# A decoder trunk's first mixer: VectorE's work in a written-out order, x loaded first, subtractions moved off GpSimd

## The chip, the cores and the metric

The kernel runs on one core of one Trainium2 chip. A core has five engines with an instruction queue each: TensorE (PE in the profile; PEld is its weight load) multiplies matrices into PSUM; VectorE (DVE) and ScalarE (ACT) work element by element and may read PSUM; GpSimd (POOL) does so on SBUF alone; SyncE (SP) issues DMA loads and stores, as the others also can. An engine runs its own queue in order and waits for the others by semaphores. The metric is device time in microseconds (us): the median of several runs; lower is better.

## The reference, cut to what matters

The program is a trunk of two decoder layers over 1024 tokens of width 1024, all in float32. Each layer is a mixer and an MLP, and in front of each stands an RMSNorm whose result is scaled and shifted by vectors made from a conditioning vector c:

```python
cond = jax.nn.silu(c)
mod = cond @ w_ada[i] + b_ada[i]                      # 6 vectors of 1024 per layer
sh1, sc1, gt1, sh2, sc2, gt2 = jnp.split(mod, 6, axis=-1)
h = rmsnorm(x, g) * (1.0 + sc1) + sh1
# layer 0's mixer (latent attention)
cq  = rmsnorm(h @ w_dq, g_q)                          # 384 wide
ckv_kr = h @ w_dkv                                    # 256 of a latent, 64 of a key
ckv, k_rope = rmsnorm(ckv_kr[..., :256], g_kv), rope(ckv_kr[..., 256:], positions)
q  = (cq @ w_uq)   # 8 heads, 128 plain + 64 rotary
kv = (ckv @ w_ukv) # 8 heads, 128 of a key + 128 of a value
```

Causal attention and an output product follow, then the MLP; layer 1 has a sliding-window mixer. The change lies in the way from x, c and the weights to the first heads of layer 0: the first mixer's entrance.

## The kernel before, in words

Activations lie transposed: a tile has 128 of the 1024 channels on its partitions and 512 tokens (half of them) along it, so h is eight chunks d = 0 to 7 for each of two halves. Precision near float32 comes from pairs: `split` rounds a tile to a TensorE type (the high part, a copy on ScalarE, mostly) and subtracts it from the source (the rest, one subtraction); `mm` then does three products, high by high, high by rest and rest by high. So every operand of a product costs a copy and a rest on some engine.

The entrance, in `run`: loads of constants, x's first half (four loads of 512 KB), and, one set per chunk, two tiles of w_ada and one of w_down (768 wide). VectorE multiplies a w_ada tile by the row of cond and adds it up along the row (`ada_sum`, L391): a column of the modulation; two columns and `ada_finish` (L399, L402) give a chunk's shift and gain. x is squared on ScalarE (L448), the squares added on VectorE (L452), and `rstd` (L461 to L468) sums over the channels by a product with ones on TensorE, then takes a logarithm and an exponential on ScalarE and a correction on VectorE: the factor. Each chunk of the first half is normed by `modulated` (VectorE times the factor, L481; ScalarE scale and shift, L482; ScalarE rounds; GpSimd takes the rest, L192), its weights are split by `down_weights` (the rest on VectorE for k = 0, 2, 4, on GpSimd otherwise, L224 for odd k), and 18 products go into six PSUM banks: three tiles of the query latent (0, 1, 2), two of the key and value latent (3, 4), one of the rotary key (5). The second half's x is loaded at k = 2, squared at k = 4, its factor made at k = 6, and its eight chunks are normed after the loop, ahead of the first half's latents.

`mla` then makes the first half's latents (each with an `rstd` of its own) and key rotation, multiplies the second half's eight chunks by tiles 5, 4, 3, later 2, 0 and 1, with the first pieces between: R (rotary queries, `mla_rope`), V (values), P (a head's plain queries and keys, `mla_head`). What comes later of these pieces is given out by `Fill`, which lets pieces run step by step in front of the score unit where they are due. Weights that come later are loaded by `Weights` and split by `weights` (rest on GpSimd). The remaining columns of w_ada trickle in between the score units.

What sets the order: the program is written in one stream, and a planner puts each engine's queue in order by a simulated time, a higher place in the stream first among what is ready. So instructions of an engine need not keep the written order, unless `chain` ties them: before, that is done for SyncE's loads and for ScalarE up to the end of the first half's loop. VectorE's order is the planner's. Buffers come in rings by tag (`t`: eight tiles of 512 for temporaries, `w`: four for raw weights, `s`: 42, PSUM `S` 3, `T` 3, `A` 2), and `chain_slots` makes the first writes into a ring keep the written order.

## Time and profile before

| What | us |
|---|---|
| median of 3 runs (lowest, highest) | 2151.04 (2149.67, 2151.49) |
| profiled execution, its span | 2150.22, 2148.4 |
| TensorE busy | 2039.0 (95%) |
| VectorE busy | 1649.7 (77%) |
| ScalarE busy | 1105.5 (51%) |
| GpSimd busy | 378.1 (18%) |

The span runs from the first to the last instruction; the profiled execution is 1.8 us longer than its span. Busy times are sums of the instructions' durations with overlaps counted once; a product's end is modelled, so a busy TensorE need not be at its peak. Where an instruction follows another on its engine at once, the next one's start minus its own is what it costs there; the duration shown is a little longer. The granted clock of TensorE is a share of 2.4 GHz; the trace holds no record of it before about 36 us and shows 1.00 there.

### The profile page before, as it was taken

To read this page: it belongs to the slowest core of one execution; us is meant where nothing else is said; L and a number is where in the kernel's file an instruction comes from. 1 tells how busy PE (TensorE), PEld (TensorE's weight loads), DVE (VectorE), ACT (ScalarE), POOL (GpSimd) and SP (SyncE) were. 2 spreads that over 40 slices of the span, in tenths; PEclk is the share of its full clock that TensorE was granted. 3 is DMA by queue.
4 is the path that set the end of the run, shared out by engine and by line. 5 is a ranking of instruction groups with operands and counts; after the bars stand their busy time and mean duration, and the time that the engine had idled before them with its cause. 6 is when DMAs were issued, how large, how long until landed. Compare 5 with 4: busy or idle time off the path is not lost.

```text
span 2148.4 us, 28329 instructions
## 1 busy us (share of the span) xinstructions
PE 2039.0 (95%) x10256; PEld 1718.5 (80%) x10256; DVE 1649.7 (77%) x2747; ACT 1105.5 (51%) x1934; POOL 378.1 (18%) x360
## 2 busy tenths in 40 slices
PE   5889999999999999999998999999999999999996
PEld 3667888889788887788887888889888887788885
DVE  8897676638887775998798998967966555987796
ACT  4455556535655554443254567855655554433443
POOL 4422222230000000000022777730000000000002
PEclk9999999999999999999998999999899999999998
DMA  8233221162566667654442122362364437634522
GB/s 301 62 112 95 57 84 35 59 196 79 207 226 225 244 246 290 244 178 166 172 154 69 60 79 70 101 187 77 129 224 156 160 125 305 218 131 150 176 79 79
DMA packets 135981, 322.61 MB, mean 150 GB/s; under 512 B 12657, under 2 KB 61313, under 8 KB 135842
## 3 DMA queue, kind: packets, MB, share of 16 engines
q1 hardware_dynamic: 135474, 320.48, 42.7%
q8 instruction: 80, 1.31, 0.3%
q14 instruction: 59, 0.48, 0.1%
q0 software_dynamic: 80, 0.14, 0.0%
q10 hardware_dynamic: 288, 0.20, 0.0%
HBM read 236.61 MB, written 84.15 MB: 149 GB/s over the span
## 4 chain that ended last, share of the span: by engine, by line
PE 74%; DVE 14%; ACT 4%; issue 3%; DMA 3%; POOL 2%; SPq 0%; DVEq 0%; POOLq 0%; ACTq 0%
PE S L230 28%; PE A L230 20%; PE T L230 19%; DVE s L192 4%; DMA w<-w_ada 1%; PE S L1238 1%; PE T L1267 1%; POOL s L192 1%; ACT s L189 1%; PE T L1000 1%; PE A L461 1%; DVE t L481 1%; DVE t L477 1%; DVE w L391 1%; DVE s L191 1%
## 5 line engine op out<-in xcount | busy, mean ns | idle before, releaser
L230 PE MATMUL S<-s,s 128*128 128x512 f32 (+3 forms) x3464 | 782.5, 379 | 14.3 <-DVE s L192 5.9
L230 PEld LDWEIGHTS S<-s,s 128*128 128x128 f32 x3464 | 626.4, 191 | 133.9 <-DVE s L192 9.1
L230 PE MATMUL A<-s,s 128*128 128x512 f32 (+3 forms) x3072 | 628.1, 354 | 17.6 <-DVE s L192 5.8
L230 PEld LDWEIGHTS A<-s,s 128*128 128x128 f32 x3072 | 500.3, 191 | 97.6 <-DVE s L192 9.5
L230 PE MATMUL T<-s,s 128*128 128x512 f32 (+1 forms) x2352 | 522.8, 378 | 24.9 <-ACT s L189 14.7
L230 PEld LDWEIGHTS T<-s,s 128*128 128x128 f32 x2352 | 420.4, 191 | 113.6 <-ACT s L189 18.6
L189 ACT CAST s<-s 128x1024 fp32r<-128x1024 f32 (+2 forms) x324 | 273.7, 899 | 309.6 <-DVE s L699 160.7
L192 DVE TENSOR_TENSOR s<-s,s 128x1024 fp32r<-128x1024 f32 (+2 forms) x316 | 325.8, 1063 | 13.8 <-ACT s L189 12.0
L192 POOL TENSOR_TENSOR s<-w,s 128x1024 fp32r<-128x1024 f32 (+3 forms) x53 | 124.3, 2352 | 671.8 <-ACT s L189 670.9
L189 ACT CAST s<-w 128x1024 fp32r<-128x1024 f32 (+3 forms) x184 | 171.3, 949 | 21.9 <-DVE w L522 5.0
L192 DVE TENSOR_TENSOR s<-w,s 128x1024 fp32r<-128x1024 f32 (+2 forms) x131 | 139.8, 1087 | 50.6 <-ACT s L189 49.3
L650 DVE TENSOR_TENSOR t<-S,t 128x512 f32<-128x512 f32 x96 | 65.8, 687 | 115.8 <-PE S L230 115.8
L651 ACT ACTIVATE t<-t 128x512 f32<-128x512 f32 x96 | 60.6, 632 | 128.4 <-DVE t L650 128.4
L1437 POOL TENSOR_TENSOR s<-s,t 128x256 f32<-128x256 f32 (+1 forms) x10 | 11.5, 1175 | 640.1 <-PE S L230 632.5
L779 DVE SCALAR_TENSOR_TENSOR s<-S,mod,s 128x512 f32<-128x512 f32 (+1 forms) x102 | 72.5, 715 | 41.3 <-PE S L230 40.9
L192 DVE TENSOR_TENSOR s<-T,s 128x512 fp32r<-128x512 f32 (+2 forms) x156 | 91.6, 602 | 12.6 <-ACT s L189 12.2
L391 DVE SCALAR_TENSOR_TENSOR s<-s,s 128x1024 f32<-128x1024 f32 x72 | 90.6, 1271 | 10.9 <-DMA s<-w_ada 10.6
L189 ACT CAST s<-T 128x512 fp32r<-128x512 f32 (+2 forms) x156 | 76.1, 523 | 42.8 <-PE T L1267 21.6
L605 DVE TENSOR_TENSOR s<-s,s 128x1024 f32<-128x1024 f32 x64 | 77.0, 1221 | 16.4 <-DMA t<-s 13.0
L985 POOL TENSOR_SCALAR s<-s,n 128x128 f32<-128x128 f32 (+3 forms) x64 | 51.0, 798 | 184.8 <-DVE n L984 162.2
L652 ACT ACTIVATE s<-t 128x512 f32<-128x512 f32 x128 | 79.7, 630 | 2.7
L699 DVE TENSOR_TENSOR s<-s,s 128x1024 f32<-128x1024 f32 x64 | 77.5, 1216 | 0.2
(151 smaller groups left out, 2048.7 us busy)
## 6 DMA issues: line engine op xcount, KB each, us to landing
t<-s SPq DMA_DIRECT2D x112, 512.0 KB, 2.8
s<-t SPq DMA_DIRECT2D x112, 512.0 KB, 5.2
s<-w_ada SPq DMA_DIRECT2D x72, 512.0 KB, 6.5
w<-w_ff SPq DMA_DIRECT2D x64, 512.0 KB, 4.4
s<-w_ff SPq DMA_DIRECT2D x64, 512.0 KB, 5.2
w<-w_ada SPq DMA_DIRECT2D x24, 512.0 KB, 3.6
w<-w_qkv SPq DMA_DIRECT2D x20, 512.0 KB, 3.5
w<-w_o SPq DMA_DIRECT2D x16, 512.0 KB, 3.5
```

The costliest lines, as they stand in the source:

```text
L189: he.copy(hi, src)
L191: he.tensor_copy(hi, src)
L192: le.tensor_tensor(out=lo, in0=src, in1=hi.bitcast(F32), op=ALU.subtract)
L230: self.nc.tensor.matmul(ps, lhsT=a, rhs=b, start=first and i == 0, stop=last and i == 2, skip_group_check=more)
L391: self.nc.vector.scalar_tensor_tensor(out=t, in0=t, scalar=1.0, in1=cond, op0=ALU.mult, op1=ALU.mult, accum_out=self.mod[layer][:, c:c + 1])
L605: nc.vector.tensor_tensor(out=out, in0=x, in1=y, op=ALU.subtract)
L650: nc.vector.tensor_tensor(out=v, in0=ps, in1=v, op=ALU.add)
L651: nc.scalar.activation(v, v, AF.Relu)
L652: nc.scalar.activation(q[r, z][:, a * HALF:(a + 1) * HALF], v, AF.Square)
L699: nc.vector.tensor_tensor(out=out, in0=x, in1=y, op=how)
L779: ins = nc.vector.scalar_tensor_tensor(out=t, in0=ps, scalar=self.modcol(layer, 5, d), in1=t, op0=ALU.mult, op1=ALU.add).ins
L985: nc.gpsimd.tensor_scalar(out=s[:, :W], in0=s[:, :W], scalar1=sm, scalar2=1.0, op0=ALU.mult, op1=ALU.mult)
```

## The change

x's four loads stand in front of everything on SyncE, and the five constants are loaded from ScalarE's queue. Twelve products of a tile of ones by itself are put on TensorE at the start. `squares` makes all squares first and adds only some of them (three at the first half, four at the second), and hands the others to `rstd` as they are. The raw w_down tile is loaded with the two w_ada tiles of its chunk. The first half's loop is written anew, with `first_norm` in three steps (product with the factor; ScalarE makes the high part and the full value in two passes; VectorE takes the rest), all of w_down's rests on VectorE, and VectorE's instructions from the squares on tied in the written order, like ScalarE's from the start. The second half's x is loaded at k = 3, squared and added at k = 4 to 6.

In `mla` the second half's chunks are normed by the same `first_norm`, one at a time, each followed by its products with tiles 3 and 4, and the first half's latents and key rotation stand between chunks 1 and 2, 2 and 3, 4 and 5. Tiles 5, 2, 0, 1 follow; P of head 0 comes before tile 0, V after it, and P of head 1 in front of the second half's query latent. The rests of w_vr, w_qk and w_o0 and the rotary product in `mla_rope` go from GpSimd to VectorE, the scale of the sine table to ScalarE.

```diff
@@ weights
-        self.split(t, w, nc.scalar, nc.gpsimd)
+        self.split(t, w, nc.scalar, nc.gpsimd if name in ("w_qkv", "w_v", "w_o1") else nc.vector)
@@ down_weights
-        le = nc.vector if k % 2 == 0 and k < 6 else nc.gpsimd
+        le = nc.vector
@@ setup
-        self.cT, _ = ld(nc.sync, "cT", [P, ND])
-        self.vec, _ = ld(nc.sync, "vec", [P, 66])
-        self.positions, first = ld(nc.scalar, "positions", [P, 256], I32)
-        self.ident, second = ld(nc.scalar, "ident", [P, P])
-        self.b_ada, _ = ld(nc.sync, "b_ada", [P, 96])
+        self.cT = ld(nc.scalar, "cT", [P, ND])
+        self.positions = ld(nc.scalar, "positions", [P, 256], I32)
+        self.vec = ld(nc.scalar, "vec", [P, 66])
+        self.ident = ld(nc.scalar, "ident", [P, P])
+        self.b_ada = ld(nc.scalar, "b_ada", [P, 96])
@@ rope_rows
-        nc.gpsimd.tensor_scalar(out=self.sin, in0=self.sin, scalar1=self.v(1), scalar2=1.0, op0=ALU.mult, op1=ALU.mult)
+        nc.scalar.activation(self.sin, self.sin, AF.Copy, scale=self.v(1))
@@ squares
+        sq = [self.slot() for _ in xs]
+        for t, x in zip(sq, xs):
+            nc.scalar.activation(t, x, AF.Square)
+        for t in sq[1:direct]:
+            nc.vector.tensor_tensor(out=sq[0], in0=sq[0], in1=t, op=ALU.add)
+            yield
+        yield [t[:, a * HALF:(a + 1) * HALF] for t in [sq[0]] + sq[direct:] for a in range(2)]
@@ new
+    def first_norm(self, d, x, rs, h, hf):
+        t = self.half()
+        nc.vector.tensor_tensor(out=t, in0=x, in1=rs, op=ALU.mult)
+        yield
+        hi, lo = h[hf, d] = self.halfpair()
+        a, sh = self.gain[0][:, d:d + 1], self.modcol(0, 0, d)
+        nc.scalar.activation(hi, t, AF.Identity, scale=a, bias=sh)
+        nc.scalar.activation(t, t, AF.Identity, scale=a, bias=sh)
+        yield
+        nc.vector.tensor_tensor(out=lo, in0=t, in1=hi.bitcast(F32), op=ALU.subtract)
+        yield
+    def mla_down_chunk(self, banks, h, w, k):
+        for i, (a, b) in enumerate(((0, 0), (1, 0), (0, 1))):
+            for t in (5, 4, 3, 0, 1, 2):
+                self.nc.tensor.matmul(banks[t], lhsT=w[k][t][a], rhs=h[0, k][b], start=k == 0 and i == 0,
+                                      stop=k == ND - 1 and i == 2)
@@ mla_rope
-        nc.gpsimd.tensor_tensor(out=sw, in0=sw, in1=self.sin[:, ts], op=ALU.mult)
+        nc.vector.tensor_tensor(out=sw, in0=sw, in1=self.sin[:, ts], op=ALU.mult)
@@ mla
-        self.mla_latent("ckv", rkv, 37, 0)
-        self.mla_key_rope(banks[5], 0)
-        self.mla_latent("cq", rcq, 34, 0)
-        banks = self.down_banks()
-        down([(k, t) for k in range(ND) for t in (5, 4, 3)])
+        for k in range(ND):
+            whole(norm[k])
+            down([k], (3, 4))
+            if k == 1:
+                self.mla_latent("ckv", rkv, 37, 0)
+            if k == 2:
+                self.mla_key_rope(old, 0)
+                banks[5] = self.tps()
+            if k == 4:
+                self.mla_latent("cq", rcq, 34, 0)
         rkv = self.mla_raw(self.KV, banks)
+        down(range(ND), (5,))
...
+        down(range(ND), (2,))
         self.mla_latent("ckv", rkv, 37, 1)
+        whole(piece("P", 0, 0))
+        down(range(ND), (0,))
         whole(piece("V", 0, 0))
+        down(range(ND), (1,))
         rcq = self.mla_raw(self.CQ, banks)
-        whole(piece("P", 0, 0))
+        whole(piece("P", 1, 0))
         self.mla_latent("cq", rcq, 34, 1)
@@ run
+        xs, x = half(0)
+        self.setup()
+        warm = self.sps()
+        for _ in range(12):
+            nc.tensor.matmul(warm[:, :P], lhsT=self.ones, rhs=self.ones, start=True, stop=True)
+        self.rope_tables()
+        self.cond_row()
         loads(0)
+        loads(1)
+        mark = len(nc.cur_bb.bb.instructions)
+        sums = list(self.squares(xs, 3))[-1]
+        column(0, 0)
+        rs = self.rstd(sums, D)
+        column(0, 1)
         banks = self.down_banks()
+        norm = {0: self.first_norm(0, x[0], rs, h, 0)}
+        next(norm[0])
+        w.append(self.down_weights(0, raw[0][1]))
+        next(norm[0])
         loads(2)
         for k in range(ND):
+            if k + 1 < ND:
+                column(k + 1, 0)
+                next(norm[k])
+                norm[k + 1] = self.first_norm(k + 1, x[k + 1], rs, h, 0)
+                next(norm[k + 1])
+                column(k + 1, 1)
+            else:
+                next(norm[k])
+            self.mla_down_chunk(banks, h, w, k)
+            if k + 1 < ND:
+                next(norm[k + 1])
+                w.append(self.down_weights(k + 1, raw[k + 1][1]))
...
+            if k == 4:
+                more = self.squares(x1s, 4)
+            if k >= 4 and k < 7:
+                next(more)
...
+            if k == 6:
+                rs1 = self.rstd(next(more), D)
         self.chain(self.loaded)
+        scope(mybir.EngineType.Activation, 0)
+        scope(mybir.EngineType.DVE, mark)
```

`column(d, a)` is one `ada_sum`, with `ada_finish` behind the second of a pair; `scope` ties an engine's instructions from a place in the stream on.

## Rows read from the trace of the kernel before

**Rows 1.** Stretch, length, busy us (instructions) of PE, PEld, DVE, ACT, POOL; clock, DMA share, GB/s.

```profile
0.00:76.00 76.00, 47.40 (x160) 32.42 (x160) 67.78 (x108) 38.66 (x51) 37.92 (x34) 0.98 0.72 251
76.00:140.00 64.00, 52.96 (x221) 39.63 (x221) 54.89 (x84) 31.81 (x55) 19.88 (x10) 0.97 0.21 68
140.00:440.00 300.00, 281.15 (x1742) 246.41 (x1741) 198.84 (x577) 168.23 (x363) 84.15 (x84) 0.99 0.23 73
```

**Rows 2.** Chain of work that ended last, 0 to 330 us: start us, us, what.

```profile
35.03 3.38 DVE s L391 x4
```

**Rows 3.** In order of time, from 0: start us, us, engine, line, operation, tiles, [idle].

```profile
1.19 0.45 ACTq L274 DMA_DIRECT2D ident<-ident  x1
...
2.13 2.02 SPq L1351 DMA_DIRECT2D s<-xT  x4
...
9.14 0.68 DVE L313 COPY s<-T 128x512 f32<-128x512 f32 x1
...
12.36 1.06 ACT L448 ACTIVATE s<-s 128x1024 f32<-128x1024 f32 x1 [1.41 <-DMA s<-xT]
```

**Rows 4.** Instructions in order of time, sums of the first RMSNorm.

```profile
20.29 3.78 PE L461 MATMUL A<-s,ones 128*128 128x512 f32 x4 [11.67 <-DVE s L452]
...
24.11 0.69 ACT L463 ACTIVATE t<-A,eps 128x512 f32<-128x512 f32 x1 [7.50 <-PE A L461]
```

**Rows 5.** TensorE's instructions from 60 us, and busy time with granted clock of 60 to 62.

```profile
60.09 2.93 PE L461 MATMUL A<-s,ones 128*128 128x512 f32 x3 [2.28 <-DVE s L452]
...
60.00:62.00 2.00, 1.91 (x3) 0.88 (x4) 2.00 (x2) 0.00 (x0) 1.70 (x1) 0.53 0.04 12
```

**Rows 6.** VectorE's instructions in order of time, 17 to 30 us.

```profile
17.01 1.22 DVE L452 TENSOR_TENSOR s<-s,s 128x1024 f32<-128x1024 f32 x1
18.15 0.95 DVE L192 TENSOR_TENSOR s<-w,s 128x768 fp32r<-128x768 f32 x1
19.02 1.22 DVE L452 TENSOR_TENSOR s<-s,s 128x1024 f32<-128x1024 f32 x1
...
20.41 1.22 DVE L391 SCALAR_TENSOR_TENSOR s<-s,s 128x1024 f32<-128x1024 f32 x1
...
21.56 1.22 DVE L391 SCALAR_TENSOR_TENSOR s<-s,s 128x1024 f32<-128x1024 f32 x1
...
23.09 1.22 DVE L391 SCALAR_TENSOR_TENSOR s<-s,s 128x1024 f32<-128x1024 f32 x1
...
28.02 2.50 DVE L481 TENSOR_TENSOR t<-s,t 128x512 f32<-128x512 f32 x4
```

**Rows 7.** ScalarE's instructions in order of time, at 31 and 75 us.

```profile
31.49 0.83 ACT L221 CAST s<-w 128x768 fp32r<-128x768 f32 x1
...
75.02 0.80 ACT L482 ACTIVATE t<-t,mod,gain 128x512 f32<-128x512 f32 x1
75.73 0.70 ACT L479 ACTIVATE t<-t,mod 128x512 f32<-128x512 f32 x1
```

**Rows 8.** TensorE's instructions in order of time, the first half's last chunk.

```profile
71.80 2.20 PE L230 MATMUL T<-s,s 128*128 128x512 f32 x9
...
73.84 2.20 PE L230 MATMUL S<-s,s 128*128 128x512 f32 x9
```

**Rows 9.** VectorE's and GpSimd's instructions in order of time, at 122 us.

```profile
122.66 2.72 DVE L477 SCALAR_TENSOR_TENSOR t<-s,vec,t 128x512 f32<-128x512 f32 x2
122.77 2.05 POOL L192 TENSOR_TENSOR s<-w,s 128x640 fp32r<-128x640 f32 x1 [7.73 <-ACT s L189]
```

**Rows 10.** Instructions in order of time, latents of the first and second half.

```profile
84.30 0.68 DVE L439 TENSOR_TENSOR t<-t,t 128x512 f32<-128x512 f32 x1
...
89.71 1.41 DVE L477 SCALAR_TENSOR_TENSOR t<-s,vec,t 128x512 f32<-128x512 f32 x2
...
134.51 1.42 PE L461 MATMUL A<-t,ones 128*128 128x512 f32 x2
```

**Rows 11.** GpSimd's groups by shape, 140 to 500 us: busy us, mean ns, idle before.

```profile
L921 POOL TENSOR_TENSOR t<-t,s 128x512 f32<-128x512 f32 x7 | 9.1, 1294 | 11.6 <-ACT t L920 11.6
```

More of the change, by code (lines that the diff above doesn't have):

```diff
@@ L440, in square_sums, with squares @@
         return acc
-    def squares(self, xs):
+    def squares(self, xs, direct):
         nc = self.nc
-        acc = None
-        for x in xs:
-            sq = self.slot()
-            nc.scalar.activation(sq, x, AF.Square)
-            if acc is None:
-                acc = sq
-            else:
-                nc.vector.tensor_tensor(out=acc, in0=acc, in1=sq, op=ALU.add)
-        return [acc[:, a * HALF:(a + 1) * HALF] for a in range(2)]
+        sq = [self.slot() for _ in xs]
[5 more added lines that the diff above has]
+        yield [t[:, a * HALF:(a + 1) * HALF] for t in [sq[0]] + sq[direct:] for a in range(2)]
     def rstd(self, acc, width):
@@ L1354, in half @@
             return xs, [t[:, a * HALF:(a + 1) * HALF] for t in xs for a in range(2)]
-        raw = {}
+        raw, w = {}, []
         def loads(d):
-            raw[d] = [self.ada_load(2 * d + a) for a in range(2)]
-        def columns(d):
-            for a in range(2):
-                self.ada_sum(2 * d + a, raw[d][a], self.row)
-            self.ada_finish(0, 2 * d, 2)
-        xs, x = half(0)
-        loads(0)
-        sq = self.squares(xs)
-        w = [self.down_weights(0)]
-        rs = self.rstd(sq, D)
@@ L1372, in run, with column, scope @@
-        columns(0)
+            raw[d] = [self.ada_load(2 * d + a) for a in range(2)], self.load(io["w_down"][d], 768)
+        def column(d, a):
+            self.ada_sum(2 * d + a, raw[d][0][a], self.row)
+            if a:
+                self.ada_finish(0, 2 * d, 2)
+        def scope(engine, first):
+            self.chain([i for i in nc.cur_bb.bb.instructions[first:] if i.engine == engine])
+        xs, x = half(0)
+        self.setup()
+        warm = self.sps()
+        for _ in range(12):
+            nc.tensor.matmul(warm[:, :P], lhsT=self.ones, rhs=self.ones, start=True, stop=True)
@@ L1395, in run @@
+            if k >= 4 and k < 7:
+                next(more)
+            if k == 3:
                 self.rope_rows()
+            if k == 6:
+                rs1 = self.rstd(next(more), D)
         self.chain(self.loaded)
-        self.chain([i for i in nc.cur_bb.bb.instructions if i.engine == mybir.EngineType.Activation])
-        rkv, rcq = self.mla_raw(self.KV, banks), self.mla_raw(self.CQ, banks)
-        for d in range(ND):
-            self.modulated(0, 0, d, x1[d], rs1, h, HALF)
+        scope(mybir.EngineType.Activation, 0)
@@ L1410, in run @@
         rest = project(0, right)
-        self.mla(h, w, banks, rkv, rcq, rest)
+        self.mla(h, w, banks, [self.first_norm(d, x1[d], rs1, h, 1) for d in range(ND)], rest)
         for _ in rest:
```

58 lines of the change are left out of this document (20 added, 38 removed).

## The prediction, made before the changed kernel ran

> **What bounds the kernel now.** I read the busy time by stretch first, then the chain of waits, and last the order of instructions in the first 140 us. From 140 us on TensorE is the busiest engine by far (281 of 300 us), so the end is late by what TensorE idles. By stretch [rows 1] that is 76 - 47.4 = 28.6 us up to 76 us, 11.0 us from 76 to 140, and 18.9 us over the next 300. The change works in the first two stretches, with a thin tail in the third. In the first stretch VectorE is busy 67.8 of 76 us; the chain stays on it for long pieces, such as its columns of w_ada [rows 2]. So VectorE's time, its work plus its waits, sets when the first mixer gets going. The sum is made against the profiled execution: 2150.22 us, of which 2148.4 span. The median of the runs is 2151.04, 0.8 above it.
>
> **x first, constants on the ScalarE queue.** x's four loads are issued at 2.13 us, behind three small loads on SyncE [rows 3]; those go, x starts at about 0.74 and the fourth square, now at 12.36, at about 10.97. ScalarE issues three more small loads at 0.45 us each before its table load and the exponential, so the row of cond, copied out by 9.82 us now, comes about 1.3 us later, near 11.1. That is the bad end of this edit; it holds nothing but VectorE's small work, which the two remaining adds come behind. I put the end of the last add at 13.4 (12.1 to 14.5).
>
> **The sums of the first RMSNorm.** One add of 1.14 us goes, and two more 512-wide halves go through the ones matmul: 8 passes for 4. At 20 us four passes took 3.78 us [rows 4], so eight take about 7.4 and ScalarE's logarithm starts at 20.8; from it to the first use of the factor now takes 24.11 to 28.02, 3.9 us [rows 4, 6]. The factor is there at 24.7 instead of 28.0: 3.3 us won. Those passes run at half speed: at 60 us, after TensorE had idled 2.28 us, three take 2.93, and the granted clock there reads 0.53, the 1.2 GHz level [rows 5]. The twelve new products at the start and the eight transposes behind them end with cond's row, some 2 us before these sums, so I keep the half speed; at 2.4 GHz the eight passes cost 3.6 us less, and that end is kept for the range. The Trainium skill (TensorE: Matmul & The Clock Gate, What's actually happening) says that the throttled state is the default and recent activity releases it. By that rule the new products would pay if nothing idle lay between, 3.6 us; the fall at 60 us speaks against it.
>
> **The first half's eight chunks in a fixed VectorE order.** This is the step that decides. Undisturbed start-to-start times [rows 6]: a column of w_ada 1.15 us (20.41 to 21.56), a column with the finish of its pair 1.53 (21.56 to 23.09), the 768-wide rest of a weight 0.87 (18.15 to 19.02), a 1024-wide add 1.14 (17.01 to 18.15), a 512-wide product 0.62 (2.50 for four); a 512-wide rest is put at 0.61. Written in order, VectorE does per chunk: rest of weight k+1, first column of k+2, rest of h of chunk k+1, product of k+2, second column and finish of k+2: 0.87 + 1.15 + 0.61 + 0.62 + 1.53 = 4.78 us. No row of before shows such a fixed order, so what it waits for is worked out. The weight's rest needs ScalarE's copy of that weight, and in ScalarE's equally fixed order the copy stands behind the two passes over chunk k+1, which need the gain that VectorE's finish has just made. Two such passes start 0.71 us apart and the copy takes 0.83 [rows 7], hand-offs 0.1: 0.71 + 0.71 + 0.83 + 0.1 = 2.35 us in which VectorE stands, with the next column, the next rest and the next product queued behind, and TensorE behind those. A chunk takes 7.1 us. The bounds are 4.78 (wait wholly hidden) and 7.3 (odd chunks cut the rest in three 256-wide pieces). TensorE needs 18 products, nine of which start 2.04 us before the next nine [rows 8]: 0.227 each, 4.1 us, so it is not the limit.
>
> From the factor at 24.7: column and finish 1.53, product 0.62, rest 0.87 (copied early, no wait), column 1.15, rest 0.61, product 0.62, column and finish 1.53 give the first full cycle a start at 31.6. Six cycles of 7.2 lead to 74.8; two adds of the second half's squares and the wait for those squares on ScalarE put 3.3 more into them: 78.1. In the last cycle the second half's sums stand in VectorE's order ahead of the last rest of h: wait and weight rest 3.4, third add 1.1, four passes 2.5 (1.9 to 3.8), 3.9 to the factor, 0.6 for the rest, six products and their end 1.6: 13.1, and the first half ends near 91 us. Now the last nine products start at 73.84 and end at 76.04 [rows 8]. This stage loses 15 us, the 3.3 won included. What speaks the other way is that now GpSimd slows VectorE: two products with x took 2.72 us beside a GpSimd rest of 2.05 us [rows 9], against 1.41 for two without one [rows 10]. The sum above already has every VectorE instruction at its undisturbed time.
>
> **The second half between the latents.** TensorE's work from there through the sums of the last latent: 144 + 9 + 30 products of 512 columns at 0.227 us, 24 of 256 at half that, four latents' sums of two passes at half of 0.9: 41.5 + 2.7 + 3.6 = 47.8 us, with the second head's piece (15 products, 3.4 us) now in front. Now these stages run from 76.04 to the sums that start at 134.51 and take 1.42 [rows 10], 59.9 us for 44.4 us of work, 15.5 idle. In the new text the chunks' temporaries and the latents' share one ring of eight, taken in the order written: chunk 2 comes behind the first latent, chunks 5 to 7 behind the second. From the last add of a latent to its first product with the factor takes 84.30 to 89.71, 5.4 us [rows 10], with copies and squares before it about 8. Behind two such waits TensorE has the six tiles of the chunks that are there: two chunks (8.2 us) behind the first, three (12.3 us) behind the second, so most is covered, if the planner places them so. I take 13 us idle (6 to 20; before has 15.5). Point of equal work: 91 + 47.8 + 13 = 151.8, against 135.9 + 3.4 = 139.3 now: 12.5 late.
>
> **Rests and the rotary product off GpSimd.** Each of the eight rotary products leaves GpSimd (1.3 us) [rows 11] for about 0.6 on VectorE; the 20 weights' rests go too, at times scaled by width from the 0.87 of 768. VectorE takes on some 20 us in all (8 x 0.74 + 4 x 1.0 + 8 x 1.14 + 8 x 0.6), spread over 300 us in which it is busy 199 [rows 1], so that is hidden by its free third; should it come due at a score unit, up to 5 us are lost. Of the 18.9 us that TensorE idles there I take 4 back (0 to 12), since rests come sooner and VectorE no longer runs beside them. The sign that is multiplied into the sine table, now on ScalarE, waits there for a load, and the passes over chunk 5 are queued behind it; the tables are made three chunks earlier, so it costs nothing, or 3 us if that load is late.
>
> Sum: 12.5 - 4 = 8.5 late, about 2159 on the profiled 2150.22, and the same within its half microsecond on the median.
>
> **The rivals.** (a) Faster: GpSimd's absence is worth more than the waits. Place: from about 76 us on, where the trace shows VectorE at nearly half speed beside GpSimd [rows 9]; if the second half runs with 3 us idle instead of 13 and 10 of the 18.9 us come back, the sum is 12.5 - 10 - 10 = -7.5: 2143. It decides from the point where the last latent's sums come before 143 us. For it: VectorE is busy 54.9 of 64 us in that stretch. Against it: the two latents' waits are TensorE idle whatever VectorE's speed. The Trainium skill (GPSIMD Engine Reference, Specifications) says that GpSimd shares its memory interfaces with VectorE instructions of two inputs; this trace agrees, 2.72 against 1.41 us.
> (b) Faster: the order does not come out as I read it, and ScalarE copies weights ahead of the two passes. VectorE then never waits, chunks take 4.8, and 7 x 2.3 = 16 us of the forecast go: 2143. Against it: the text writes the copy behind.
> (c) No change: the waits are there, but the planner fills TensorE behind them (6 us idle) and 6 us come back later: 12.5 - 7 - 6, 2150 to 2151.
> (d) Slower still: TensorE, idle in three places per 7 us chunk, drops to 1.2 GHz as at 60 us [rows 5]; then 18 products take 8, a chunk at least that, 7 x 0.9 more and a slow restart of each stage: 9 us on top, 2168. Against it: work is there in each of the three places, so no single idle time is much over 2 us.
>
> **How the numbers follow.** Forecast 0.40 (own range 2153 to 2166), (a) 0.14, (b) 0.12, (c) 0.20, (d) 0.14. About 0.2%, 4.3 us, is what can be told from no change: faster 0.26, same 0.20, slower 0.54. The range 2138 to 2173 takes in the rivals' times, with the full-speed sums below and the 20 us idle second half above; 0.1 is left out on each side.
>
> **What would show it.** Right: in the profile after, VectorE waits of over 2 us for ScalarE's weight copy in each of chunks 1 to 7; first-half products some 7 us apart per chunk, ending near 90; sums of the first norm starting near 13.5 and taking over 6 us; second-half products with gaps around two latents; TensorE busy in the first 76 us clearly under 47. Wrong: chunks of 5 us, a first half done before 80, no VectorE wait on the copy, or the last latent's sums before 143 us.

## The result, and the profile after

The changed kernel takes 2177.9 us (median of 4 runs, 2177.07 to 2178.58); the kernel before took 2151.26 in the same comparison. The ratio is 1.0123 (95%: 1.011 to 1.0135): 26.5 us slower, where 8.5 were forecast, in a range that ended at 2173. The direction was right, the size wrong.

First the stretches of [rows 1], now of the changed kernel.

```profile
0.00:76.00 76.00, 44.41 (x147) 31.95 (x148) 44.13 (x98) 29.98 (x36) 3.37 (x12) 0.80 0.71 241
76.00:140.00 64.00, 45.01 (x146) 31.37 (x145) 43.02 (x74) 28.21 (x43) 0.00 (x0) 0.84 0.14 46
140.00:440.00 300.00, 285.41 (x1730) 247.84 (x1729) 221.63 (x610) 173.35 (x372) 49.08 (x63) 0.99 0.20 65
```

In the first two stretches VectorE is busy 87 us instead of 123, GpSimd 3 instead of 58, and TensorE, is busy 11 us less: nobody is the bottleneck by work, so most of the time goes in waits. TensorE's granted clock is lower too: 0.87 from 36 to 76 us, for 0.96 before; the 0.98 of [rows 1] cannot be compared, since that trace has no record of it ahead of 36 us. In the third stretch TensorE is busy 4.3 us longer than before.

The start, instructions in order of time (start us, us, engine, line; in brackets the idle time before and what ended it). It answers to [rows 3, 4].

```profile
0.74 2.50 SPq L1375 DMA_DIRECT2D s<-xT  x4
...
9.46 0.35 DVE L342 TENSOR_SCALAR s<-s,vec 128x256 f32<-128x256 f32 x1 [3.69 <-DMA vec<-vec]
...
10.78 2.75 PE L308 MATMUL T<-ident,s 128*128 128x128 f32 x8 [4.98 <-DMA ident<-ident]
...
11.96 1.06 ACT L444 ACTIVATE s<-s 128x1024 f32<-128x1024 f32 x1 [0.58 <-DMA s<-xT]
...
15.44 2.54 DVE L446 TENSOR_TENSOR s<-s,s 128x1024 f32<-128x1024 f32 x2
...
18.04 5.61 PE L456 MATMUL A<-s,ones 128*128 128x512 f32 x8 [4.51 <-DVE s L446]
...
23.68 0.69 ACT L458 ACTIVATE t<-A,eps 128x512 f32<-128x512 f32 x1 [10.67 <-PE A L456]
```

x is issued 1.4 us earlier, yet its last square starts only 0.4 us earlier (11.96 for 12.36). Two small constants (vec and ident), issued at 1.69 and 2.17 us among x's loads, land after 7.7 and 8.5 us; VectorE and TensorE stand for them, the small work on cond and on the position tables comes late, and the adds behind it end at 18.0 instead of the forecast 13.4.

One chunk of the first half's loop, VectorE and ScalarE in order of time.

```profile
48.60 0.16 DVE L398 SCALAR_TENSOR_TENSOR gain<-mod,vec 128x1 f32<-128x1 f32 x1
48.79 0.81 ACT L488 ACTIVATE s<-t,mod,gain 128x512 fp32r<-128x512 f32 x1 [1.48 <-DVE gain L398]
...
49.64 0.81 ACT L489 ACTIVATE t<-t,mod,gain 128x512 f32<-128x512 f32 x1
50.36 0.81 ACT L220 CAST s<-w 128x768 fp32r<-128x768 f32 x1
51.21 1.10 DVE L223 TENSOR_TENSOR s<-w,s 128x256 fp32r<-128x256 f32 x3 [2.45 <-ACT s L220]
...
52.22 1.22 DVE L387 SCALAR_TENSOR_TENSOR s<-s,s 128x1024 f32<-128x1024 f32 x1
...
53.36 0.69 DVE L491 TENSOR_TENSOR s<-t,s 128x512 fp32r<-128x512 f32 x1
...
53.97 0.69 DVE L484 TENSOR_TENSOR t<-s,t 128x512 f32<-128x512 f32 x1
...
54.57 1.22 DVE L387 SCALAR_TENSOR_TENSOR s<-s,s 128x1024 f32<-128x1024 f32 x1
...
56.03 0.16 DVE L398 SCALAR_TENSOR_TENSOR gain<-mod,vec 128x1 f32<-128x1 f32 x1
```

The circle is closed: the gain (L398) lets ScalarE make two passes, behind these comes the copy of the next weight, for that VectorE stands 2.45 us, and only then does it make the next gain, 7.43 us after the last.

The same kernel, 28 to 98 us: what VectorE and ScalarE waited for (us in total, times, longest).

```profile
DVE s L223 <- ACT s L220: 13.8, 4, 6.4
...
ACT s L378 <- DMA s<-trig: 7.8, 1, 7.8
DVE s L192 <- ACT s L189: 7.4, 3, 2.5
```

Seven waits for the copy. One of them is 6.4 us: ScalarE itself stood for the sine table's load (L378), so from chunk 4 to chunk 5 it took 11.3 us instead of 7.4. The end of the first half, some of the second half, and the last latent's sums answer to [rows 8, 10]:

```profile
97.63 1.48 PE L886 MATMUL S<-s,s 128*128 128x512 f32 x3
...
112.64 1.42 DVE L472 SCALAR_TENSOR_TENSOR t<-s,vec,t 128x512 f32<-128x512 f32 x2
...
114.31 0.68 DVE L484 TENSOR_TENSOR t<-s,t 128x512 f32<-128x512 f32 x1
...
115.89 0.73 PE L229 MATMUL T<-s,s 128*128 128x512 f32 x2 [3.38 <-ACT s L488]
...
117.98 7.05 PE L229 MATMUL T<-s,s 128*128 128x512 f32 x16 [1.36 <-DVE t L914]
...
129.88 5.60 PE L229 MATMUL S<-s,s 128*128 128x512 f32 x24
...
131.50 1.41 DVE L472 SCALAR_TENSOR_TENSOR t<-s,vec,t 128x512 f32<-128x512 f32 x2
...
134.76 0.68 DVE L484 TENSOR_TENSOR t<-s,t 128x512 f32<-128x512 f32 x1
...
168.47 1.12 PE L456 MATMUL A<-t,ones 128*128 128x512 f32 x2
```

The first half's last product starts at 98.49 and, with 0.227 us for it, ends near 98.7 (75.9 before; ends of other kernels' first halves below are taken the same way; the 76.04 of [rows 8] is the profile's modelled end). Five traces with this same first half (this one, e3, e5, e9 and e13) end it between 97.1 and 101.8, so a place in one trace is good to about 2 us. Chunk 2's product (114.31) follows the first latent's (112.64), chunk 5's (134.76) the second's (131.50), as read from the ring. The last latent's sums end at 169.6, against 139.3 for equal work in the kernel before: 30.3 us late, of which 22.8 were lost in the first half and 7.5 in the second. The medians are 26.6 apart, so 3.7 come back later; that is a difference and was not read from a row.

TensorE from 98 to 170 us, to compare with the second stretch of [rows 1]:

```profile
98.00:170.00 72.00, 58.96 (x229) 43.26 (x228) 50.77 (x84) 40.30 (x67) 0.00 (x0) 0.89 0.14 45
```

It stands 13.0 us here (72.00 less 58.96), and 11.0 in the stretch of before. What grew more is the time of the products: between the first half's end and the last latent's sums TensorE is busy 57.9 us for the 47.8 us of products that the prediction counted (before 48.9 for 44.4). The sixteen products from 117.98 on start 0.43 us apart, the 24 from 129.88 on 0.23. The granted clock is 0.54 from 98 to 108 us and 0.68 from 118 to 128, which mixes the 1.2 and the 2.4 GHz level, and 1.00 from 128 to 150; before the first fall TensorE had stood 3.9 us (up to 96.55), at the second 3.4 and 1.4 us (up to 115.89 and 117.98).

### The profile page after: what moved, and what is told of

Same layout as the page of the kernel before. It is cut to its first block, busy times and chain, and to the rows that moved or that the text cites. A ratio compares the mean times of both kernels' runs of the same rounds, so it can differ in the third digit from the quotient of the medians.

```text
span 2175.3 us, 28372 instructions
## 1 busy us (share of the span) xinstructions
PE 2056.6 (95%) x10284; PEld 1729.5 (80%) x10284; DVE 1653.8 (76%) x2791; ACT 1113.3 (51%) x1943; POOL 284.0 (13%) x306
## 4 chain that ended last, share of the span: by engine, by line
PE 74%; DVE 14%; ACT 6%; DMA 4%; issue 2%; POOL 0%; SPq 0%; DVEq 0%; ACTq 0%; POOLq 0%
PE S L229 28%; PE A L229 21%; PE T L229 20%; DVE s L192 4%; DMA w<-w_ada 1%; ACT s L189 1%; PE S L1265 1%; PE T L1016 1%; DVE s L191 1%; PE T L1294 1%; ACT t L936 1%; DMA s<-w_ff 1%; PE A L456 1%; DVE s L387 1%; DVE t L472 1%
## 5 line engine op out<-in xcount | busy, mean ns | idle before, releaser
L229 PE MATMUL S<-s,s 128*128 128x512 f32 (+3 forms) x3392 | 763.8, 378 | 14.7 <-ACT t L1194 3.8
L229 PEld LDWEIGHTS S<-s,s 128*128 128x128 f32 x3392 | 610.7, 190 | 133.2 <-DVE s L192 5.4
L229 PE MATMUL T<-s,s 128*128 128x512 f32 (+1 forms) x2280 | 508.4, 379 | 21.4 <-ACT s L189 8.5
L229 PEld LDWEIGHTS T<-s,s 128*128 128x128 f32 x2280 | 409.2, 192 | 106.9 <-ACT s L189 11.0
L192 DVE TENSOR_TENSOR s<-s,s 128x1024 fp32r<-128x1024 f32 (+2 forms) x316 | 326.1, 1064 | 14.2 <-ACT s L189 12.5
L192 DVE TENSOR_TENSOR s<-w,s 128x1024 fp32r<-128x1024 f32 (+3 forms) x152 | 161.6, 1082 | 68.3 <-ACT s L189 67.1
L192 POOL TENSOR_TENSOR s<-w,s 128x1024 fp32r<-128x1024 f32 x32 | 80.6, 2525 | 613.3 <-ACT s L189 612.3
L189 ACT CAST s<-T 128x512 fp32r<-128x512 f32 (+2 forms) x156 | 76.4, 524 | 50.9 <-PE T L1016 22.4
L387 DVE SCALAR_TENSOR_TENSOR s<-s,s 128x1024 f32<-128x1024 f32 x72 | 87.3, 1220 | 7.3 <-DMA s<-w_ada 7.3
```

Source lines behind the costliest of these rows:

```text
L189: he.copy(hi, src)
L192: le.tensor_tensor(out=lo, in0=src, in1=hi.bitcast(F32), op=ALU.subtract)
L229: self.nc.tensor.matmul(ps, lhsT=a, rhs=b, start=first and i == 0, stop=last and i == 2, skip_group_check=more)
L387: self.nc.vector.scalar_tensor_tensor(out=t, in0=t, scalar=1.0, in1=cond, op0=ALU.mult, op1=ALU.mult, accum_out=self.mod[layer][:, c:c + 1])
```

## The experiments

Each was timed beside the kernel before on one chip, but not all on the same one, so runs are compared by their ratios. Against before is (ratio - 1) x 2151 us; "against the changed kernel" below is the difference of two ratios, good to about 4 us.

| run | median us | ratio to before (95%) | against before, us |
|---|---|---|---|
| changed kernel | 2177.9 | 1.0123 (1.0110 to 1.0135) | +26.5 |
| e1 copy first | 2166.0 | 1.0061 (1.0045 to 1.0078) | +13.1 |
| e2 sine on GpSimd | 2176.6 | 1.0109 (1.0094 to 1.0125) | +23.4 |
| e3 norms first | 2172.5 | 1.0093 (1.0078 to 1.0108) | +20.0 |
| e4 rests on GpSimd | 2189.1 | 1.0169 (1.0154 to 1.0184) | +36.4 |
| e5 columns later | 2178.6 | 1.0119 (1.0099 to 1.0138) | +25.6 |
| e6 constants back | 2175.4 | 1.0104 (1.0088 to 1.0119) | +22.4 |
| e7 before, off GpSimd | 2138.3 | 0.9936 (0.9921 to 0.9951) | -13.8 |
| e8 five edits | 2148.8 | 0.9991 (0.9981 to 1.0000) | -1.9 |
| e9 old second half | 2170.3 | 1.0079 (1.0061 to 1.0098) | +17.0 |
| e10 four edits | 2149.8 | 0.9986 (0.9977 to 0.9996) | -3.0 |
| e11 no written order | 2163.1 | 1.0041 (1.0028 to 1.0055) | +8.8 |
| e12 = e10, no order | 2156.4 | 1.0014 (1.0004 to 1.0023) | +3.0 |
| e13 split norms | 2177.3 | 1.0120 (1.0105 to 1.0135) | +25.8 |
| e14 = e10, split norms | 2141.8 | 0.9951 (0.9934 to 0.9967) | -10.5 |

**e1, the weight's copy ahead of the two passes**

```diff
-                next(norm[k + 1])
                 w.append(self.down_weights(k + 1, raw[k + 1][1]))
+                next(norm[k + 1])
```

> The changed kernel with one pair of statements exchanged: in each chunk of the first half ScalarE's copy of the next weight is written ahead of the two passes over the next chunk of x instead of behind them. Theory (the wait decides): VectorE stands some 2.4 us per chunk for that copy, because the copy is queued behind two passes that need the gain VectorE has just made; with the copy in front, that wait falls to under 0.5 us, a chunk takes about 5.0 to 5.4 us instead of 7.4, the first half ends near 84 us instead of 98.7, and the time is about 2162 to 2164. Rival (TensorE's clock decides): with 18 products at half speed, 8 us per chunk, the chunk stays at 7 us or more and the time stays at 2176 to 2178 although the VectorE wait is gone. Second rival (the wait moves): VectorE now waits as long for the passes themselves, at its product; chunk near 6.5 us, 2171.

Measured: 2166.0 us, 13.3 less by ratio. Waits of 28 to 90 us in VectorE's queue, and ScalarE at the sine table:

```profile
DVE s L223 <- ACT s L220: 10.7, 2, 9.4
```

```profile
50.39 10.68 SPq L376 DMA_DIRECT2D s<-trig  x8
...
63.16 1.15 ACT L378 ACTIVATE s<-s,vec 128x1024 f32<-128x1024 f32 x1 [10.56 <-DMA s<-trig]
```

Five of seven waits for the copy are gone and chunks take 4.9, 5.8 and 5.1 us; what is left in the row is nearly all the 9.4 us behind the sine's load, which now takes 14.0 us from chunk 4 to 5. So the first half ends at 90.4, not at 84. The wait is shown as the cause of the long chunks. TensorE's clock is not: at 0.92 in 36 to 66 us, about as in the changed kernel (0.94), the loop ran at 5 us a chunk.

**e2, the sine table's sign back on GpSimd**

```diff
-        nc.scalar.activation(self.sin, self.sin, AF.Copy, scale=self.v(1))
+        nc.gpsimd.tensor_scalar(out=self.sin, in0=self.sin, scalar1=self.v(1), scalar2=1.0, op0=ALU.mult, op1=ALU.mult)
```

> The changed kernel with the product of sign and sine table given back to GpSimd, so that ScalarE no longer waits there for the tables' load. Theory: the 7.84 us that ScalarE stood for that load held the passes over chunk 5 and so one VectorE cycle; chunk 4 to 5 takes 7.4 us instead of 11.3, and 3.5 to 4 us of the total go: about 2174. Rival: the cycle of chunk 5 was late for another reason (its squares of the second half, or the loads of x), and the time stays within 1 us of 2177.9.

Measured: 2176.6 us; 3.0 less by ratio, within the 4 us. In its trace chunk 4 to 5 takes 7.3 us and the first half ends 2.5 us earlier, but the last latent's sums start at 168.0 for 168.5. The wait is confirmed; taken away alone it hardly reaches the end.

**e3, the second half's normalisations first**

```diff
         for k in range(ND):
             whole(norm[k])
+        for k in range(ND):
             down([k], (3, 4))
```

> The changed kernel with the second half's eight normalisations all written ahead of its products and latents, as in the kernel before; the products stay spread between the latents. Theory: chunk 2 no longer stands behind the first latent and chunks 5 to 7 no longer behind the second, so TensorE's idle time between the end of the first half (98.7 us) and the last latent's sums falls from 23 us to about 13 to 15, and the time is about 2168 to 2170. Rival (the columns of w_ada in VectorE's queue decide there): the normalisations then wait behind the same columns, the idle time stays over 20 us and the time stays at 2176 or more.

Measured: 2172.5 us, 6.5 less by ratio. The first half ends at 100.3, the last latent's sums end at 165.0: 64.7 us for 47.8 of counted work, 17 beyond it for 23 (standing 9.7 for 13.0, products 55.0 for 57.9). The chunks behind the latents cost some 6 us, not all of it.

**e4, rests and rotary product back on GpSimd** (in the changed kernel)

```diff
-        self.split(t, w, nc.scalar, nc.gpsimd if name in ("w_qkv", "w_v", "w_o1") else nc.vector)
+        self.split(t, w, nc.scalar, nc.gpsimd)
...
-        nc.vector.tensor_tensor(out=sw, in0=sw, in1=self.sin[:, ts], op=ALU.mult)
+        nc.gpsimd.tensor_tensor(out=sw, in0=sw, in1=self.sin[:, ts], op=ALU.mult)
```

> The changed kernel with the 20 weights' rests and the eight rotary products given back to GpSimd, everything else as changed. Theory: the part taken off GpSimd is worth what the stretch of 300 us behind the entrance showed, 3 to 4 us, so the time rises to 2181 to 2182. Rival: those 3.7 us come from the later start of that stretch (more is ready when TensorE gets there), and the time stays within 1 us of 2177.9. Second rival: VectorE is the busier engine here, GpSimd gives relief, and it falls below 2176.

Measured: 2189.1 us, 9.9 more by ratio: every theory fell, and the first, which had the sign right, was too small. Its stretch 170 to 470 us, then that of the changed kernel:

```profile
170.00:470.00 300.00, 279.05 (x1724) 243.25 (x1723) 199.18 (x582) 168.45 (x366) 83.21 (x83) 0.99 0.22 71
```

```profile
170.00:470.00 300.00, 286.62 (x1759) 250.50 (x1758) 217.51 (x604) 170.37 (x367) 50.61 (x64) 0.99 0.24 79
```

TensorE does 7.6 us less with GpSimd than without. The longest of its waits there (166 to 470 us), and below it GpSimd's group of rests, three widths together:

```profile
PE A L229 <- POOL s L192: 4.2, 3, 2.3
```

```profile
L192 POOL TENSOR_TENSOR s<-w,s 128x640 fp32r<-128x640 f32 (+2 forms) x13 | 26.2, 2021 | 35.4 <-ACT s L189 35.4
```

**e7, the kernel before with that part alone**

```diff
-        self.split(t, w, nc.scalar, nc.gpsimd)
+        self.split(t, w, nc.scalar, nc.gpsimd if name in ("w_qkv", "w_v", "w_o1") else nc.vector)
...
-        nc.gpsimd.tensor_tensor(out=sw, in0=sw, in1=self.sin[:, ts], op=ALU.mult)
+        nc.vector.tensor_tensor(out=sw, in0=sw, in1=self.sin[:, ts], op=ALU.mult)
```

> The kernel before with one part of the change alone: the 20 weights' rests and the eight rotary products on VectorE instead of GpSimd. The kernel with that part undone rose by 11 us, where the comparison of the two traces had shown 3.7 us won behind the entrance. Theory A (this part is worth about 11 us by itself, and the two stages of the entrance lose some 37 instead of 30): about 2140. Theory B (it is worth 3 to 4 us here, and undoing it in the changed kernel cost more because there the entrance ends later and GpSimd's rests run into the scores): 2147 to 2148.

Measured: 2138.3 us, 13.8 less than before: theory A, and the fastest kernel here. Its stretches, which answer to [rows 1], and VectorE where [rows 9] stood:

```profile
0.00:76.00 76.00, 47.69 (x160) 33.24 (x160) 67.78 (x109) 39.24 (x52) 38.79 (x35) 0.91 0.73 251
76.00:140.00 64.00, 56.46 (x241) 43.01 (x240) 55.03 (x91) 31.87 (x55) 7.91 (x5) 0.97 0.19 60
140.00:440.00 300.00, 288.30 (x1780) 252.71 (x1779) 216.71 (x600) 170.67 (x366) 51.03 (x63) 1.00 0.27 85
```

```profile
123.13 0.82 DVE L192 TENSOR_TENSOR s<-w,s 128x640 fp32r<-128x640 f32 x1
123.87 1.41 DVE L477 SCALAR_TENSOR_TENSOR t<-s,vec,t 128x512 f32<-128x512 f32 x2
```

The rest takes 0.82 us on VectorE for 2.05 on GpSimd, and the two products behind it 1.41 for the 2.72 they took beside GpSimd: VectorE takes the work on and is done with both sooner. This place is the worst one: the other seven rests of that width took 1.56 to 1.58 us on GpSimd. TensorE gains 3.5 us in 76 to 140 and 7.2 in the next 300. How much of that comes from rests that are ready sooner, and how much from VectorE running alone, was not told apart.

**e5, the last columns of w_ada behind the second latent**

```diff
...
-            self.ada_sum(i, t, cond)
+            ins = self.ada_sum(i, t, cond)
+            if i == 16:
+                self.follow(ins, self.lead)      # VectorE's last instruction of the second half's query latent
...
```

> The changed kernel with the last columns of w_ada, the ones that wait for a load one after another, kept in VectorE's queue behind the second latent instead of ahead of its squares and products. Theory (those four loads, 8 us of VectorE waiting between 91 and 140 us, push the latents out): TensorE's idle time between 98.5 us and the last latent's sums falls from 23 us to 16 to 19, the time to 2171 to 2175. Rival (VectorE would otherwise have waited there for the latents' own inputs, since chunks stand behind latents): under 1.5 us, 2176.5 to 2178.

Measured: 2178.6 us, unchanged. VectorE's waits from 91 to 140 us, first in the changed kernel, then in this one (its line numbers are two higher):

```profile
DVE w L387 <- DMA w<-w_ada: 8.0, 3, 3.6
DVE t L459 <- ACT t L458: 3.6, 2, 2.4
DVE s L491 <- ACT t L489: 2.1, 2, 1.7
```

```profile
DVE t L461 <- ACT t L460: 8.0, 3, 3.1
DVE s L493 <- ACT t L491: 7.2, 4, 4.3
```

The 8.0 us for loads are gone; 9.5 us more of waiting for ScalarE stand in their place. The most striking wait of the trace was not a cause: the rival holds.

**e6, the constants back ahead of x**

```diff
-        self.cT = ld(nc.scalar, "cT", [P, ND])
+        self.cT = ld(nc.sync, "cT", [P, ND])          # vec and b_ada likewise
...
-        xs, x = half(0)
         self.setup()
+        xs, x = half(0)
```

> The changed kernel with the three constants back on SyncE's queue and the constants' loads ahead of x's. Theory (the constants, landing behind 2 MB of x, hold VectorE until 9.46 us and TensorE until 10.78 us, and by that the last add, which ended at 18.0 instead of 13.4): the first sums start 1.5 to 2.5 us earlier than 18.04, all of it reaches the end of the first half: 2175.5 to 2176.5. Rival: the last square, which then comes later with x, sets the adds, and the sums start where they did; the time stays within 1 us of 2177.9.

Measured: 2175.4 us, 4.1 less by ratio, at the edge of what can be told. The adds and the first sums (L458 here is L456 of the changed kernel):

```profile
12.79 6.10 PE L458 MATMUL A<-s,ones 128*128 128x512 f32 x8 [4.66 <-DVE s L448]
```

The sums start 5.2 us earlier, though x is issued 1.4 us later: the constants set that point. At the end of the first half 3.1 of the 5.2 are left (chunk 4 to 5, where ScalarE stands for the sine's load, takes 12.4 us here instead of 11.3), at the last latent's sums 1.5.

**e9, the second half in the order before** (the eight normalisations, both latents, then tiles 5, 4, 3 chunk by chunk, 2, 0 and 1; the second head's piece given to `Fill`)

```diff
-        for k in range(ND):
-            whole(norm[k])
-            down([k], (3, 4))
-            if k == 1:
-                self.mla_latent("ckv", rkv, 37, 0)
...
+        for d in range(ND):
+            whole(norm[d])
+        self.mla_latent("ckv", rkv, 37, 0)
+        self.mla_key_rope(banks[5], 0)
+        self.mla_latent("cq", rcq, 34, 0)
+        banks = self.down_banks()
...
-            if due > 4:
+            if due > 2:
```

> The changed kernel with its second half put back to the order of the kernel before: all eight normalisations ahead, both latents of the first half next, then the products tile by tile, the second head's piece no longer in front. Theory: against the kernel before with its rests off GpSimd (2138.3), the changed kernel loses 39.6 us, of which the first half's later end is 22.5 (98.5 against 76 us); the other 17 belong to the second half's order and its after-effects up to the first scores. With it put back: 2160 to 2164. Rival 1 (most of the 17 is an after-effect of the late first half, such as the trickled columns): 2169 to 2173, as with the normalisations alone ahead. Rival 2: the second half's order costs nothing and only the columns' waits do: 2176 or more.

Measured: 2170.3 us, 9.5 less by ratio: the theory's 17 fell, and the time lies in rival 1's range, though its reason was not tested. Counted by TensorE's products done since the start, each at a fixed duration by its width, both traces stand at 169.5 us where the changed kernel has its last latent's sums; the gain comes behind that, some 5 us by 223 us and 7 by 260 (the profiled executions are 8.0 apart). The 54 us behind, first for this kernel, then for the changed one:

```profile
169.00:223.00 54.00, 50.55 (x279) 41.87 (x278) 50.11 (x138) 30.72 (x69) 11.58 (x13) 0.97 0.39 120
```

```profile
169.00:223.00 54.00, 46.41 (x239) 37.67 (x238) 46.65 (x119) 28.35 (x63) 8.48 (x10) 0.94 0.37 114
```

TensorE is busy 4.1 us more there. So the new order costs little up to the last latent but leaves the first score units worse placed; what in them does it was not told apart.

**e8, five edits at once** (e1, e2, e3, e5, e6)

> The changed kernel with five edits at once: the weight's copy ahead of the two passes, the sign's product on GpSimd, the second half's normalisations written ahead, the last columns behind the second latent, the constants back ahead of x. In the run with the copy in front ScalarE stood 10.6 us for the sine tables, and chunk 4 to 5 took 14.0 us; so with both that wait goes too. Theory (the waits in the fixed order are the loss): 11.9 + 8 for the first two, 5.4 for the third, 1 to 4 for the last two; 2149 to 2152, and the first half ends near 81 us. Rival (TensorE's clock takes over, 18 products at half speed in 8 us per chunk): first half near 88, 2157 or more.

Measured: 2148.8 us, as the theory said; but the first half ends at 75.6, over 5 us better than expected, so behind it some 5 us were lost that the theory did not have, and the agreement of the total is partly luck.

**e10, e1 + e2 + e6 with the second half of e9**

> The changed kernel with the copy ahead of the two passes, the sign's product on GpSimd, the constants back ahead of x, and the second half in the order of the kernel before; what stays of the change is the fixed VectorE order, the first sums with one add less, the chunks' product order and the rests off GpSimd. In the run of five edits the first half ended at 75.3 us (76 before), and behind it about 11 us went against the kernel before with its rests off GpSimd. Theory (those 11 are the second half's order): 2135 to 2139, as good as 2138.3 or a little better. Rival (they come from the fixed order's after-effects, squares and columns late): 2145 or more.

Measured: 2149.8 us: the theory fell, and the time is the rival's; e14 and e12 below speak against the rival's reason. Both this kernel and e7 end the first half at 76 us and go on in the same order, and it is 10.8 us (by ratio) behind. ScalarE, of which the 76 to 90 us are filled, and the first latent's sums:

```profile
76.00:90.00 14.00, 11.20 (x43) 8.41 (x42) 8.91 (x14) 14.00 (x22) 0.00 (x0) 0.88 0.01 2
```

```profile
92.41 1.02 PE L458 MATMUL A<-t,ones 128*128 128x512 f32 x2
```

`first_norm` gives ScalarE two passes a chunk; sixteen of 0.71 us stand in front of the latent's squares, and its sums start at 92.4 instead of 84.5.

**e14 and e13, the normalisation split over three engines again**, in e10 and in the changed kernel

```diff
-        self.mla(h, w, banks, [self.first_norm(d, x1[d], rs1, h, 1) for d in range(ND)], rest)
+        self.mla(h, w, banks, [partial(self.modulated, 0, 0, d, x1[d], rs1, h, HALF) for d in range(ND)], rest)
```

> The kernel with the copy in front, the sign on GpSimd, the constants ahead and the old second half (2149.8), now also with each second-half normalisation split over three engines as in the kernel before. There the two passes keep ScalarE busy for 14.0 of the 14 us from 76 to 90 us, and the first latent's sums come 7.7 us later than in the kernel before with its rests off GpSimd (2138.3), although both end the first half at 76 us. Theory A: that wait goes and the time is 2141 to 2144. Rival B: the latents then wait for VectorE, which takes the passes' place, and the time stays above 2147.

> The changed kernel with one edit in the second half: each chunk's normalisation is split over VectorE, ScalarE and GpSimd as in the kernel before (one ScalarE pass a chunk) instead of two ScalarE passes; the order of chunks, products and latents stays as changed. Theory A (ScalarE's two passes, 13 us over eight chunks, stand in front of the latents' copies and squares and push them out): 3 to 7 us faster, 2171 to 2175. Theory B (there the chunks wait for the ring of temporaries and the columns, ScalarE is idle half of the time): within 2 us of 2177.9.

Measured: e14 2141.8 us, 7.5 less than e10 by ratio, with the first latent's sums at 87.3 (theory A). e13 2177.3 us, no change (theory B): in the changed kernel's order the second pass costs nothing that can be told. That it is hidden there by the chunks' wait for the latents' ring is the theory's reason and was not shown by itself.

**e11 and e12, VectorE's written order taken away**, in the changed kernel and in e10

```diff
-        scope(mybir.EngineType.DVE, mark)
```

> The changed kernel without the written order of VectorE's instructions in the first half; everything else, ScalarE's written order too, as changed. Theory A (the written order makes the waits): VectorE takes columns and rests that are ready while a weight's copy is awaited, chunks take 5 to 5.5 us and the time is 2160 to 2166, as with the copy in front. Theory B (ScalarE's order holds the copy behind passes that need the gain; VectorE, whatever its order, has little else that is ready): chunks stay at 7 us and the time within 3 us of 2177.9.

> The kernel with the copy in front, the sign on GpSimd, the constants ahead and the old second half, now also without VectorE's written order. If a written order costs by itself even where its waits are mended, 1 to 4 us less than with it; if it keeps the columns and rests from running ahead of the products that TensorE needs, 1 to 5 us more; if the written order is what the planner would choose anyway, the same within 1 us.

Measured: e11 2163.1 us, 17.6 less by ratio (theory A); e12 2156.4, 6.0 more than e10. VectorE in e11 before the first sums:

```profile
17.63 1.22 DVE L387 SCALAR_TENSOR_TENSOR s<-s,s 128x1024 f32<-128x1024 f32 x1
...
18.77 1.22 DVE L446 TENSOR_TENSOR s<-s,s 128x1024 f32<-128x1024 f32 x1
...
19.91 1.22 DVE L387 SCALAR_TENSOR_TENSOR s<-s,s 128x1024 f32<-128x1024 f32 x1
...
21.05 1.22 DVE L446 TENSOR_TENSOR s<-s,s 128x1024 f32<-128x1024 f32 x1
```

Free to choose, VectorE does columns between the adds, and the sums start at 22.3 instead of 18.0 (in e12 at 22.2 instead of 12.8); but the waits for the copy fall from 21.2 to 2.9 us and the first half ends at 87.3. So the written order helps where the text writes the urgent thing first (e10's sums come 9.4 us before e12's) and costs where it closes a circle with ScalarE's.

## Why the prediction was wrong

The forecast was 8.5 us late, the kernel 26.5. The point of equal work, 12.5 us late in the forecast and 30.3 in the trace, holds nearly the whole miss: 17.8 us, of which 7.7 lie in the first half and 10.1 in the term for the second half. The loop, on which the forecast was built, came out.

By ratio, the copy's place is worth 13.3, the second half's order 9.5, the constants 4.1 and the sine 3.0, 29.9 in sum; the four undone together (e10) give 29.5. That these agree so closely is partly luck: each is good to 4 us, and the constants and the sine, undone alone, bring the last latent's sums only 1.5 and 0.4 us forward. Splitting the norms gives 7.5 more (e14), 3.2 then lie between e14 and e7 and stay open. Off GpSimd gives 13.8. That 29.5 + 7.5 + 3.2 - 13.8 makes 26.4 proves nothing, since each term is the step from one kernel to the next.

| step | forecast | measured in the trace |
|---|---|---|
| last add of the first norm ends | 13.4 | 18.0 |
| factor of the first norm there | 24.7 | 27.1 |
| eight sums | 7.4 us | 5.6 us |
| one chunk | 7.1 to 7.3 us | 7.4 us |
| last cycle starts | 78.1 | 85.4 |
| first half ends | 91 | 98.7 |
| time beyond the counted 47.8 us, from there to the last latent | 13 us | 23 us |
| equal-work point, late by | 12.5 us | 30.3 us |
| back behind it | 4 us | 3.7 us, by difference |

**The loop: right.** "VectorE stands, with the next column, the next rest and the next product queued behind", 2.35 us a chunk: the trace shows 2.45, and e1 and e11 take it away for 13 and 18 us. Rival (b) fell with it: in the changed kernel the copies are not ahead.

**The start: wrong.** "That is the bad end of this edit; it holds nothing but VectorE's small work" counted the issues of the constants and left out their landing among 2 MB of x. It did set the two adds behind that work, but put its end at 11.1, where the trace has 15.4. Worth 4.6 us at the adds; the sums' faster second half gave 1.8 back. e6 shows it: 12.8 for 18.0.

**The sine: bounded too low.** "It costs nothing, or 3 us if that load is late". It was late; the cycle lost 3.9 us, and the faster the loop before it, the more (e1: 10.6 us of standing). With the start's 2.4 and six cycles slower by about 0.2 us, these make the 7.7 us by which the first half ended later than forecast.

**The second half: the step that failed most.** "So most is covered, if the planner places them so. I take 13 us idle (6 to 20)". The time beyond the counted work is 23 us. Of it TensorE stands 13.0: the cover worked behind the second latent, where 24 products run on from 129.88, and only in part behind the first, where TensorE stands 3.4 and 1.4 us. The other 10.1 are busy time beyond the 0.227 us at which the term counted every product. The forecast had set its 13 beside the 15.5 of the kernel before, of which 11.0 are standing and 4.5 such busy time. So against before the standing grew by 2.0, where a fall was forecast, and the busy time by 5.6, in stretches where the clock falls to its 1.2 GHz level; the rows show this, but no run changed the clock alone. That TensorE stood 13.0 us where 13 was forecast is luck. e3 takes 6 of the 23 away, half of it standing. Unseen was a further part, behind the latents: the order costs about 7 us more in the first score units (e9). The columns of w_ada that VectorE stood for there look like another part and are none (e5).

**Off GpSimd: the sign right, the size taken too low.** "I take 4 back (0 to 12)": alone the part gives 13.8, undone it costs 9.9. That some 3.7 came back behind the entrance, as forecast, is luck: at equal work the traces show some 9 won there by this part alone (e7) and some 7 lost to the second half's order (e9). The prediction took a share of the idle time of that stretch and left the measured pair of [rows 9], in which GpSimd takes 2.05 us for a rest and VectorE's time beside it nearly doubles, to rival (a). Such places are few: of VectorE's 24 columns from 100 to 440 us three took over 1.25 us in the kernel before, the longest 3.10, and one in e7, 1.70; the median is 1.23 in both. What VectorE takes on adds up to 23.8 us by the prediction's own terms, where it writes some 20; its busy time from 140 to 440 us rose by 22.8. The Trainium skill (GPSIMD Engine Reference, Specifications) lists the memory interfaces as shared, with contention for VectorE instructions that have two inputs in SBUF; e7's rows agree, 1.41 us for 2.72.

Of the rivals, (a) had this mechanism (10 us behind the entrance) and not the entrance's losses. (c) fell. (d) was right that TensorE falls to its 1.2 GHz level in the loop's gaps, which reach 2.9 us for the copy and 6.9 at the sine, where the prediction allowed not much over 2. But the clock does not set the chunk: the two chunks from 34.1 to 48.8 us took 7.44 and 7.28 us at a clock of 1.00 (36 to 49 us), the next 7.43 at 0.79 (49 to 57), and e1 ran at 5 us a chunk. The slow restart behind the loop, which (d) also named, is there: it is the products' part in the second half.

## What to carry to other kernels

Fixing one engine's order beside another's fixed order needs a walk around the circle: here a copy written two instructions too late cost 13 us, and exchanging two statements gave it back, while the same fixed order is worth 6 us where its waits are mended. Count for a moved load when it lands beside the others, not when it is issued. And test each part of a mixed change by itself: the part that looked least, off GpSimd, made the only clear gain (2138.3 us, 0.9936 of before), hidden by 40 us of losses in the parts beside it.

## What was not expected of the hardware

Loads of 33 to 64 KB, issued from ScalarE's queue at 1.69 to 2.66 us while four of 512 KB went out on SyncE's from 0.74 us on, took 7.7 to 8.9 us to land; 4 KB issued together with the first of the four took 2.1, and 128 KB issued 0.5 us later 3.9. In e6 the same three small loads, issued from 1.18 to 1.66 us ahead of the four, took 2.2 to 3.4. A queue of its own did not put the small loads ahead.

The twelve products at the start did not make the first norm's sums fast: of the eight passes the first five started 0.85 to 1.02 us apart and the last ones 0.43, and in e6, where TensorE no longer waits for ident and the transposes end by 8.1 us, it stood 4.66 us in front of the sums all the same, and the eight took 6.10 us.
